# Forgetting-attention layer: the last gate projections move beside the last head, the maxima run 34 units ahead, half of w_out is split in front of the last head, the constant rows come by DMA

## The chip, the cores and the metric

One Trainium2 chip, one core of it. The metric is the time of one execution on the device in microseconds, as the median of several runs. The kernel before took 1217.65 us (three runs, 1216.58 to 1218.84).

## The reference, cut to what matters

One decoder layer over 2048 tokens of width 1024. Eight heads of forgetting attention (full causal softmax with a bias from summed gate logits) and eight query heads of sliding-window attention share one normalised input and one input projection. Each head's output is multiplied by a SiLU gate; one output projection, a norm and a gated residual follow.

```python
proj = h @ w_in[l]
qa, ka, va, fa, za, qb, kb, vb, zb = jnp.split(proj, split_points, axis=-1)
...
oa = oa * jax.nn.silu(za)
...
y = jnp.concatenate([oa, ob], axis=-1) @ w_out[l]
x = x + gate[:, None, :] * rms_norm(y, g_post[l])
```

and in forgetting_attention, for a block of 128 queries:

```python
s = jnp.einsum('bhqd,bhkd->bhqk', qb, kh, preferred_element_type=jnp.float32) * scale
s = s + cb[..., None] - cum[:, :, None, :]
...
s = jnp.where(causal, s, -jnp.inf)
p = jax.nn.softmax(s, axis=-1)
return jnp.einsum('bhqk,bhkd->bhqd', p.astype(vh.dtype), vh)
```

## The kernel before, in words

Every product is made of three f16 matmuls: operands are split into a high and a low half, and high x high, high x low and low x high are summed in PSUM. The tokens lie in four chunks of 512. `hT[0..3]` holds the normalised input of each chunk, turned and split, 16 KB a partition each.

The kernel has three stages on one instruction stream per engine. First the input is normalised and turned. Then the sliding-window stage runs, with projections between its pieces. Its last piece hands over to the third stage, the forgetting attention (FoX), whose start I call the prologue. The output projection follows at the end.

**Units.** A projection of one 128-column weight group for one chunk (`proj_units`, L299) is eight units, each of three matmuls of 512 columns (L308). The list `punits` holds all of them in order, and `fill(n)` issues the next n. `qk0..qk7` are query and key of the eight FoX heads, `za0..za3` the gates of two heads each, `va3` the last values. When a chunk of `qk` is done, ACT and DVE make its high and low half (`stq`, L997 and L990) and four DMAs on SP's queue put them into the tile `T` of the head (L992 to L995; two such tiles take turns). A chunk of `za` goes through a tanh on ACT (L352) and a product on DVE (L348), and GpSimd's queue stores it to `z_d` in DRAM (L350).

**Weights.** Each group is loaded, its largest magnitude found (DVE, L212), sent through DRAM (`mx_d`, L215 and L220, GpSimd's queue) and split (ACT L246, DVE L252), so many units ahead of its first use (`add`, L902).

**Maxima.** The softmax needs a row bound per query. `munits` holds for each head 40 segments, each a matmul on `T` (L1209) and a maximum on DVE (L1212, or L1214 on the diagonal), and four short units that turn the bound into extra rows of `T` (L1166, ACT L1170, SP L1172): 44 per head (`M_HEAD`). The first `M_LEAD` = 26 are issued in the prologue, beside its last projections.

**Steps.** A head is 20 steps, each of up to 1024 scores per query row. Step s does on ACT the exponential of its scores (L1265) and the f16 high half (L1269), on DVE the low half of the step before (L1272), on TensorE the scores of the next step (L1258, L1259, on the diagonal L1261) and the values product of the step two back (`PV_LAG` = 2, L1282 to L1285). Between them stand some filling units and 2.2 maxima a step. A head's chunk ends with a division (L1289, L1291) and a store of `ona` to `o_d` on SP's queue (L1292). In heads 0 to 6 the filling units are projections. In the last head steps 0 to 7 have none, and from step 8 on the first 33 units of the output projection (L1407) fill.

**The last head before.** After its step 0 `open_out` (L1319) closes the pools of `hT` and of the staging tiles and opens those of the output stage. `w_out` is loaded in 16 pieces of 128 x 512 on SP's queue (L1342) and split, one piece a step from step 2 on, by ACT (L1347) and DVE (L1348), right after the step's exponential. The left half (pieces 0 to 7) is needed by the first product in step 9. The loads of the first two output blocks (`o_d`, L1362, and `z_d`, L1364) follow steps 4 and 6; their turning (`Out.turn`) makes ACT square and round a gated block (L1383, L1393).

**Constant rows.** `T` needs three constant values in each row of its two slots. In the prologue four small matmuls (L1157) and sixteen ACT copies of 5 x 512 (L1159) put them there.

Of the kernel before, what the change touches and what calls it, by code (L numbers as in the profile page):

```python
# [41 lines left out]
def hybrid_layer(  # L42
# [75 lines left out]
    hpx = ExitStack()  # L118
    hpool = hpx.enter_context(tc.tile_pool(name="hpool", bufs=1))
# [13 lines left out]
    hT = [hpool.tile([P, 2, KT, CH], F16, name=f"hT{i}") for i in range(NCH)]  # L133
# [517 lines left out]
    def open_fox():  # L651
# [8 lines left out]
        fx["cst"] = cst = fxv.tile([P, 2, XR], F16, name="cst")  # L660
        for ap, val in ((vt[:, :, :, 64:65], 1.0), (cst[:], 0.0), (fx["lk"][:], 0.0), (fx["lq"][0][:], 0.0),
                        (fx["lq"][1][:], 0.0), (cst[:, 0, 64:65], XA), (cst[:, 0, 65:66], XB),
                        (cst[:, 0, 68:69], XC), (cst[:, 1, 66:67], XA), (cst[:, 1, 67:68], XB)):
            V.memset(ap, val)

# [312 lines left out]
    N_SWA = len(punits)  # L978
    for ci in range(2):
        add("va3", va_units(3, ci))  # L980
# [173 lines left out]
    def const_rows(n, slot):  # L1154

        px = bk[bank()][:]
        PE.matmul(px[0:XR, 0:P], fx["cst"][:, slot // 2, :], identh[:], start=True, stop=True)  # L1157
        for c_ in range(NCH):
            after(1, lambda c_=c_: A.activation(  # L1159
                Ts[n][64:XR, slot, c_ * CH:(c_ + 1) * CH].rearrange("p (u q) -> p u q", u=4),  # L1160
                px[64:XR, 0:P].unsqueeze(1).broadcast_to([XR - 64, 4, P]), AF.Copy))
# [149 lines left out]
    M_HEAD, M_LEAD, PV_LAG = 44, 26, 2  # L1311
# [7 lines left out]
    def open_out():  # L1319
# [5 lines left out]
        stp = foxo.enter_context(tc.tile_pool(name="stpo", bufs=6, reuse_waits="tile"))  # L1325
        oxy = foxo.enter_context(tc.tile_pool(name="oxy", bufs=2, reuse_waits="tile"))
        oio["x"] = lambda: oxy.tile([P, D], F32, tag="xr", name="xr")
        oio["y"] = lambda: oxy.tile([P, D], F32, tag="yg", name="yg")
# [10 lines left out]
    def w_out_load(m):  # L1339
        k, cc = m % KT, slice((m // KT) * CH, (m // KT + 1) * CH)  # L1340
        w_raw[m] = stp.tile([P, CH], F32, tag="st", name=f"wo{m}")
# [10 lines left out]
    class Out:  # L1352
# [43 lines left out]
        def product(self, n, k):  # L1396
# [15 lines left out]
            def evac():  # L1412
                if n == 0:
                    self.y = oio["y"]()
# [179 lines left out]
```

## Time and profile before

| | us |
|---|---|
| median of three runs | 1217.65 |
| the profiled execution | 1213.1 |
| its span, first to last instruction | 1211.3 |
| TensorE busy | 1156.8 |
| DVE busy | 907.4 |
| ACT busy | 675.1 |

The page's "busy" is the time in which an engine has an instruction under way; for TensorE (PE) ends are modelled and neighbours overlap, so its rate is read from how closely instructions start. Windows are stretches of the span with the busy time of each engine, and PEclk is the share of the full TensorE clock that was granted. In the timeline, what stands in brackets is the idle time of the engine before a row and what ended it.

### The profile page before, as it was taken

To read this page: it belongs to the slowest core of one execution; us is meant where nothing else is said; L and a number is where in the kernel's file an instruction comes from. 1 tells how busy PE (TensorE), PEld (TensorE's weight loads), DVE (VectorE), ACT (ScalarE), POOL (GpSimd) and SP (SyncE) were. 2 spreads that over 40 slices of the span, in tenths; PEclk is the share of its full clock that TensorE was granted. 3 is DMA by queue.
4 is the path that set the end of the run, shared out by engine and by line. 5 is a ranking of instruction groups with operands and counts; after the bars stand their busy time and mean duration, and the time that the engine had idled before them with its cause. 6 is when DMAs were issued, how large, how long until landed. Compare 5 with 4: busy or idle time off the path is not lost.

```text
span 1211.3 us, 27309 instructions
## 1 busy us (share of the span) xinstructions
PE 1156.8 (96%) x10832; PEld 698.7 (58%) x10832; DVE 907.4 (75%) x2271; ACT 675.1 (56%) x1117; POOL 142.1 (12%) x252
## 2 busy tenths in 40 slices
PE   6789999999999999999999999999999969999996
PEld 2467546865558976555555555555555546555553
DVE  6866567686776646688888798888978787667665
ACT  2766445565655451566667666666766779433231
POOL 2011133223232210001010110010000000000000
PEclk8889999999999999999999999999999989999998
DMA  9554332323323322313334323122111146455652
GB/s 325 189 146 142 83 95 73 86 56 102 96 68 87 57 55 51 82 58 84 84 60 83 88 61 79 38 72 53 42 45 36 41 140 192 144 164 184 202 170 81
DMA packets 87668, 120.97 MB, mean 100 GB/s; under 512 B 27340, under 2 KB 63220, under 8 KB 87540
## 3 DMA queue, kind: packets, MB, share of 16 engines
q1 hardware_dynamic: 76564, 86.20, 23.8%
q0 software_dynamic: 10976, 33.03, 11.6%
q8 instruction: 85, 1.39, 0.5%
q14 instruction: 43, 0.35, 0.1%
HBM read 71.82 MB, written 25.18 MB: 80 GB/s over the span
## 4 chain that ended last, share of the span: by engine, by line
PE 80%; DVE 7%; DMA 6%; SPq 3%; ACT 2%; issue 1%; POOL 0%; DVEq 0%; ACTq 0%; POOLq 0%
PE bk L308 30%; PE bk L1407 13%; PE bk L326 7%; PE sta L1258 4%; PE sta L1259 4%; PE bk L1209 4%; PE poa L1284 2%; PE poa L1285 2%; PE poa L1282 2%; PE pxb L866 2%; PE pss L833 2%; PE pob L885 2%; DVE pha L1272 1%; DMA xt<-in_x_dram 1%; PE bk L1370 1%
## 5 line engine op out<-in xcount | busy, mean ns | idle before, releaser
L1265 ACT ACTIVATE p<-sta,lift,scl_qk 128x1024 f32<-128x1024 f32 (+2 forms) x160 | 171.9, 1075 | 128.7 <-PE sta L1259 72.7
L308 PE MATMUL bk<-hT,wh_qk 128*128 128x512 f16 x768 | 193.4, 378 | 0.6 <-DVE a_m L1212 0.6
L1407 PE MATMUL bk<-wohl,oz 128*128 128x512 f16 x768 | 172.1, 379 | 0.0
L1272 DVE TENSOR_TENSOR pha<-p,pha 128x1024 f16<-128x1024 f32 (+2 forms) x160 | 169.1, 1057 | 0.2 <-ACT pha L1269 0.2
L1212 DVE TENSOR_REDUCE a_m<-bk 128x1 f32<-128x512 f32 x192 | 130.2, 686 | 49.7 <-PE bk L1209 49.1
L1269 ACT ACTIVATE pha<-p 128x1024 f16<-128x1024 f32 (+2 forms) x160 | 148.0, 925 | 5.5 <-PE bk L1209 0.4
L1407 PEld LDWEIGHTS <-oz 128*128 128x128 f16 x768 | 74.4, 99 | 81.2
L1282 PE MATMUL poa<-vt,pha 128*128 128x65 f16 x1088 | 117.6, 194 | 1.3 <-DVE ona L1291 1.2
L1258 PE MATMUL sta<-T 128*128 128x512 f16 (+1 forms) x320 | 111.7, 349 | 7.5 <-ACT p L1265 7.3
L1285 PE MATMUL poa<-vt,pha 128*128 128x65 f16 x1088 | 117.3, 193 | 1.1 <-DVE pha L1272 1.1
L1284 PE MATMUL poa<-vt,pha 128*128 128x64 f16 x1088 | 117.7, 195 | 0.0
L308 PEld LDWEIGHTS <-wh_qk 128*128 128x128 f16 x768 | 73.0, 97 | 76.0 <-issue 1.7
L1209 PE MATMUL bk<-T 66*128 66x512 f16 (+2 forms) x320 | 110.1, 351 | 2.9 <-DMA T<-stq 2.0
L1282 PEld LDWEIGHTS <-pha 128*128 128x128 f16 x1088 | 102.3, 97 | 16.5 <-DVE ona L1291 3.0
L1259 PE MATMUL sta<-T 69*128 69x512 f16 (+1 forms) x320 | 110.8, 351 | 0.0
L1284 PEld LDWEIGHTS <-pha 128*128 128x128 f16 x1088 | 101.7, 97 | 11.3
L1285 PEld LDWEIGHTS <-pha 128*128 128x128 f16 x1088 | 101.6, 99 | 1.3 <-DVE pha L1272 1.3
L308 PE MATMUL bk<-hT,wh_za 128*128 128x512 f16 x384 | 99.4, 378 | 0.0
L308 PE MATMUL bk<-hT,wh_zb 128*128 128x512 f16 x384 | 89.9, 379 | 1.1 <-DVE wh_zb L252 1.1
L326 PE MATMUL bk<-wh_va,hT 128*128 128x128 f16 x1536 | 90.7, 219 | 0.0
L326 PEld LDWEIGHTS <-hT 128*128 128x128 f16 x1536 | 87.5, 98 | 5.0 <-issue 2.5
L308 PE MATMUL bk<-hT,wh_qb 128*128 128x512 f16 x384 | 87.2, 379 | 0.0
(493 smaller groups left out, 1890.5 us busy)
## 6 DMA issues: line engine op xcount, KB each, us to landing
wa<-in_w_ada_dram SPq DMA_DIRECT2D x16, 512.0 KB
z_d<-tz POOLq DMA_DIRECT2D x32, 256.0 KB, 3.1
T<-stq SPq DMA_DIRECT2D x64, 128.0 KB
T<-o_d SPq DMA_DIRECT2D x16, 512.0 KB
T<-z_d SPq DMA_DIRECT2D x16, 512.0 KB
xr<-in_x_dram SPq DMA_DIRECT2D x16, 512.0 KB
out_dram<-yg SPq DMA_DIRECT2D x15, 512.0 KB
xt<-in_x_dram SPq DMA_DIRECT2D x12, 512.0 KB
```

The costliest lines, as they stand in the source:

```text
L308: PE.matmul(ps, whl[:, a, k, :], hT[ci][:, b, k, :], start=(k == 0 and n == 0), stop=(k == KT - 1 and n == 2))
L326: PE.matmul(ps[:, u * P:(u + 1) * P], hT[ci][:, a, k, u * P:(u + 1) * P], whl[:, b, k, :], start=(k == 0 and n == 0), stop=(k == KT - 1 an ...
L1209: PE.matmul(mx[:, :w], T[0:XM, 0, i * P:(i + 1) * P], T[0:XM, 2, pc * CH:pc * CH + w], start=True, stop=True)
L1258: PE.matmul(self.st[:, o:o + w], T[:, 3, kb_], T[:, 1, qc], start=True, stop=False)
L1259: PE.matmul(self.st[:, o:o + w], T[0:XR, 2, kb_], T[0:XR, 0, qc], start=False, stop=not diag)
L1265: A.activation(self.p32[:, :self.w], self.st[:, :self.w], AF.Exp, scale=scl[f"qk{self.hd}"][:], bias=lift[:])
L1269: A.activation(self.ph[:, 0, :self.w], self.p32[:, :self.w], AF.Copy)
L1272: V.tensor_tensor(self.ph[:, 1, :self.w], self.p32[:, :self.w], self.ph[:, 0, :self.w], op=ALU.subtract)
L1282: PE.matmul(po[:, u, :], ph[:, 0, pq], vt[:, b, hd, 0:65], start=(self.first and n == 0 and u == 0), stop=False)
L1284: PE.matmul(po[:, u, 0:64], ph[:, 0, pq], vt[:, b, hd, 65:VW], start=False, stop=False)
L1285: PE.matmul(po[:, u, :], ph[:, 1, pq], vt[:, b, hd, 0:65], start=False, stop=(self.last and n == len(self.blocks) - 1))
L1407: PE.matmul(py, self.hl[:, i, k, :], w_slot(8 * j + k)[:, cc], start=(k == 0 and m_ == 0), stop=(k == KT - 1 and m_ == 2))
```

## The change

It has five parts.

1. **Gates.** The filling list keeps `qk1..qk7` and the gates of heads 0 to 6 in heads 0 to 6 (336 units up to `N_LAST` instead of 352). The last two chunks of `za3` (16 units) follow `N_LAST` and are issued two a step in steps 0 to 7 of the last head. In the list, `qk7`'s chunks stand between those of `za3`, and the weights of the `za` groups are prepared against a due place moved by four units (for `za3` by 20).
2. **Maxima.** `M_LEAD` is 34 instead of 26: eight more units are issued in the prologue, from 14 units before `N_QK0` on instead of 10. Each head's key rows are made at steps 0 and 1 instead of 2 and 3.
3. **w_out.** `open_out` happens when all but the last chunk of `qk7` and nothing late is pending (it comes in step 12 of the head before the last). It closes only `hT[0]` and `hT[1]`. The left half's eight pieces are split in steps 14 to 19 of that head and in steps 1 and 3 of the last head, the right half's in steps 9 to 16 of the last head. Each piece is loaded once, two steps ahead (before, piece 0 was loaded twice, after steps 0 and 1).
4. **Buffers.** `hT[2]` and `hT[3]` stay. The right half's pieces land in `hT[3]`, and the two residual and two output tiles of the output stage lie in `hT[2]`. The staging pool there has 4 tiles instead of 6.
5. **Constant rows.** One matmul and one ACT copy, 40 units before the end of the sliding-window list, make a row tile `crow`. In the prologue three DMAs per `T` spread it, on SP's queue for `T[0]` and on ACT's queue for `T[1]`.

```diff
-    for hd in range(1, 9):
+    for hd in range(1, 7):
         for part in range(6):
             if part in (3, 5):
                 add(f"za{(hd - 1) // 2}", za_units(hd - 1, (part - 3) // 2))
-            elif hd < 8:
+            else:
                 add(f"qk{hd}", qk_units(hd, (0, 1, 2, 0, 3)[part]))
+    add("qk7", qk_units(7, 0))
+    add("za3", za_units(6, 0))
+    add("qk7", qk_units(7, 1))
+    add("qk7", qk_units(7, 2))
+    add("za3", za_units(6, 1))
+    N_OPEN = len(punits)
+    add("qk7", qk_units(7, 3))
+    N_LAST = len(punits)
+    for n in range(2):
+        add("za3", za_units(7, n))
...
-            at = len(punits) - (24 if key[:2] == "za" else 0)
+            at = len(punits) - {"za3": 4}.get(key, 20 if key[:2] == "za" else 0)
...
-    def const_rows(n, slot):
-        px = bk[bank()][:]
-        PE.matmul(px[0:XR, 0:P], fx["cst"][:, slot // 2, :], identh[:], start=True, stop=True)
-        for c_ in range(NCH):
-            after(1, lambda c_=c_: A.activation(
-                Ts[n][64:XR, slot, c_ * CH:(c_ + 1) * CH].rearrange("p (u q) -> p u q", u=4),
-                px[64:XR, 0:P].unsqueeze(1).broadcast_to([XR - 64, 4, P]), AF.Copy))
+    def const_rows(n, eng):
+        for slot, r0, r1 in ((0, 64, 66), (2, 66, 68), (0, 68, 69)):
+            eng.dma_start(Ts[n][r0:r1, slot, :].rearrange("p (u q) -> p u q", q=P),
+                          fx["crow"][r0:r1, :].unsqueeze(1).broadcast_to([r1 - r0, NB, P]))
...
-    M_HEAD, M_LEAD, PV_LAG = 44, 26, 2
+    M_HEAD, M_LEAD, PV_LAG = 44, 34, 2
...
-            if mi < M_LEAD and pos[0] >= N_QK0 - 10:
+            if mi < M_LEAD and pos[0] >= N_QK0 - 14:
...
-        p0, p_tot = pos[0], len(punits) - pos[0]
+        p0, p_tot = pos[0], N_LAST - pos[0]
-        w_at = {r: [r - 2] if r < 10 else [8, 9] if r == 10 else [r - 1] for r in range(2, 17)}
+        w_at, opened = {}, False
...
+            if hd == 7 and r < 8:
+                npn = N_LAST + (len(punits) - N_LAST) * (r + 1) // 8 - pos[0]
...
-            if hd == 7 and r == 0:
+            if not opened and pos[0] >= N_OPEN and (r >= 14 or not late):
+                while late:
+                    tick()
                 open_out()
-            if hd == 7:
-                for m in (w_at[2] if r == 1 else []) + w_at.get(r + 2, []):
-                    w_out_load(m)
+                opened = True
+                here = list(range(s + 2, 7 * NS))[:KT]
+                here += [7 * NS + n for n in (1, 3, 5, 7, 8)][:KT - len(here)] + [7 * NS + n for n in range(9, 17)]
+                w_at = {t: [m] for m, t in enumerate(here)}
+            for m in w_at.get(s + 2, []):
+                w_out_load(m)
```

Three places show how the instructions move. First ACT's row at the start of the prologue, before (`T` are the tiles of two heads, `rw` the key rows of head 0, `stq` the chunks of `qk0`):

```order
L1098 ACTIVATE wsq,a_m<-wsq 128x256
L1159 ACTIVATE T_6650<-bk_134 5x512 x4
L1159 ACTIVATE T_6650<-bk_136 5x512 x4
L1159 ACTIVATE T_6651<-bk_135 5x512 x4
L1159 ACTIVATE T_6651<-bk_6625 5x512 x4
L1170 ACTIVATE rw<-bk_6626 48x128
L997 ACTIVATE stq<-bk_134 128x512
```

The same place now; the sixteen copies are gone and three DMA issues stand there, the other three being in SP's row:

```order
L1118 ACTIVATE wsq,a_m<-wsq 128x256
L1177 DMA T_6657<-crow 2x16x128 x2
L1177 DMA T_6657<-crow 1x16x128
L1187 ACTIVATE rw<-bk_137 48x128
L1006 ACTIVATE stq<-bk_138 128x512
```

Second, ACT's row from step 19 of head 6 into the last head, before (`p` is an exponential, `pha` its high half, `wohl` a split piece of w_out):

```order
L1265 ACTIVATE p_14138<-sta,lift,scl_qk_11693 128x384
L1269 ACTIVATE pha<-p_14138 128x384
L1265 ACTIVATE p_14184<-sta,lift,scl_qk_12666 128x896
L1269 ACTIVATE pha<-p_14184 128x896
L1265 ACTIVATE p_14245<-sta,lift,scl_qk_12666 128x384
L1269 ACTIVATE pha<-p_14245 128x384
L1170 ACTIVATE rw<-bk_6625 8x128
L1265 ACTIVATE p_14279<-sta,lift,scl_qk_12666 128x1024
L1347 ACTIVATE wohl<-wo_14275,wsc 128x512
L1269 ACTIVATE pha<-p_14279 128x1024
```

The same engine now, in steps 14 to 17 of head 6; the splits begin eight steps sooner, one a step:

```order
L1282 ACTIVATE p_13905<-sta,lift,scl_qk_11874 128x1024
L1368 ACTIVATE wohl<-wo_13864,wsc 128x512
L1286 ACTIVATE pha<-p_13905 128x1024
L1006 ACTIVATE stq<-bk_6632 128x512
L1282 ACTIVATE p_13953<-sta,lift,scl_qk_11874 128x1024
L1368 ACTIVATE wohl<-wo_13903,wsc 128x512
L1286 ACTIVATE pha<-p_13953 128x1024
L1282 ACTIVATE p_14000<-sta,lift,scl_qk_11874 128x1024
L1368 ACTIVATE wohl<-wo_13951,wsc 128x512
```

Third, SP's queue around the first loads of w_out, before (`o_d_72<-ona` is the store of head 6's last chunk):

```order
L1342 DMA wo_14243<-in_w_out_dram 128x512
L1172 DMA T_6651<-rw 2x4x128
L1292 DMA o_d_72<-ona 128x4x64
L1342 DMA wo_14275<-in_w_out_dram 128x512
L1342 DMA wo_14277<-in_w_out_dram 128x512
L1342 DMA wo_14319<-in_w_out_dram 128x512
L1292 DMA o_d_69<-ona 128x4x64
```

The same queue now; the second and third load stand behind the store of head 6's third chunk, and the eighth behind that of its last:

```order
L1359 DMA wo_13864<-in_w_out_dram 128x512
L1309 DMA o_d_71<-ona 128x4x64
L1359 DMA wo_13903<-in_w_out_dram 128x512
L1359 DMA wo_13951<-in_w_out_dram 128x512
L1001 DMA T_6657<-stq 64x2x512
```

```order
L1189 DMA T_6657<-rw 2x4x128
L1359 DMA wo_14095<-in_w_out_dram 128x512
L1359 DMA wo_14181<-in_w_out_dram 128x512
L1309 DMA o_d_72<-ona 128x4x64
L1359 DMA wo_14262<-in_w_out_dram 128x512
```

In both fences a load that stood behind a store of `ona` keeps one in front of it, but now only three of the left half's eight do.

More of the change, by code (lines that the diff above doesn't have):

```diff
@@ L131, in hybrid_layer @@
     swc = swx.enter_context(tc.tile_pool(name="swc", bufs=1))
-    hT = [hpool.tile([P, 2, KT, CH], F16, name=f"hT{i}") for i in range(NCH)]
+    hT = [(hpool if i < 2 else hlate).tile([P, 2, KT, CH], F16, name=f"hT{i}") for i in range(NCH)]
     cosT = swc.tile([P, S], F32, name="cosT")
@@ L659, in open_fox, with const_turn @@
         fx["lq"] = [fxv.tile([P, LW], F16, name=f"lq{n}") for n in range(2)]
-        fx["cst"] = cst = fxv.tile([P, 2, XR], F16, name="cst")
+        fx["cst"] = cst = fxv.tile([P, XR], F16, name="cst")
+        fx["crow"] = fxv.tile([P, P], F16, name="crow")
         for ap, val in ((vt[:, :, :, 64:65], 1.0), (cst[:], 0.0), (fx["lk"][:], 0.0), (fx["lq"][0][:], 0.0),
-                        (fx["lq"][1][:], 0.0), (cst[:, 0, 64:65], XA), (cst[:, 0, 65:66], XB),
-                        (cst[:, 0, 68:69], XC), (cst[:, 1, 66:67], XA), (cst[:, 1, 67:68], XB)):
+                        (fx["lq"][1][:], 0.0), (cst[:, 64:65], XA), (cst[:, 65:66], XB),
+                        (cst[:, 66:67], XA), (cst[:, 67:68], XB), (cst[:, 68:69], XC)):
             V.memset(ap, val)
+    def const_turn():
+        px = bk[bank()][:]
+        PE.matmul(px[0:XR, 0:P], fx["cst"][:], identh[:], start=True, stop=True)
+        after(1, lambda: A.activation(fx["crow"][64:XR, :], px[64:XR, 0:P], AF.Copy))
     def va_units(j, ci):
@@ L1472, in hybrid_layer @@
         V.tensor_copy(cmask[:, 3 * P:], dmask[:])
-        for n in range(2):
-            for slot in (2, 0):
-                const_rows(n, slot)
-                tick()
+        const_rows(0, SP)
+        const_rows(1, A)
         key_limbs(0)
```

28 lines of the change are left out of this document (16 added, 12 removed).

## The prediction

> **What bounds the kernel now.** I read the page first, then windows cut at the stages of FoX, then the timeline at the two places where TensorE stops. In the page's row each engine has its busy time:
>
> ```profile
> PE 1156.8 (96%) x10832; PEld 698.7 (58%) x10832; DVE 907.4 (75%) x2271; ACT 675.1 (56%) x1117; POOL 142.1 (12%) x252
> ```
>
> TensorE is the bound on average, so time can only come from where it stops. The windows show where; per row: length, busy time of PE, its weight loads, DVE, ACT, POOL, then the granted clock.
>
> ```profile
> core 0: us, PE busy (x) PEld busy (x) DVE busy (x) ACT busy (x) POOL busy (x), PEclk, DMA share, GB/s
> 441.30:444.70 3.40, 1.26 (x15) 0.77 (x12) 2.76 (x15) 3.38 (x9) 0.71 (x1) 1.00 0.14 43
> ...
> 559.90:630.20 70.30, 68.95 (x705) 39.47 (x702) 61.11 (x136) 46.27 (x54) 6.12 (x10) 1.00 0.27 66
> 630.20:907.40 277.20, 276.58 (x2809) 159.35 (x2806) 236.09 (x523) 183.05 (x212) 20.80 (x33) 1.00 0.28 62
> ...
> 957.30:973.50 16.20, 14.46 (x225) 9.76 (x222) 15.31 (x30) 13.93 (x18) 0.54 (x1) 1.00 0.09 34
> 973.50:977.50 4.00, 2.98 (x37) 1.44 (x34) 3.61 (x10) 1.17 (x1) 0.00 (x0) 1.00 0.09 24
> 977.50:982.60 5.10, 0.00 (x0) 0.00 (x0) 2.05 (x5) 2.81 (x4) 0.00 (x0) 0.65 0.50 166
> 982.60:992.70 10.10, 9.86 (x102) 6.20 (x102) 10.01 (x19) 8.44 (x12) 0.00 (x0) 0.67 0.53 158
> 992.70:1009.90 17.20, 14.32 (x152) 10.00 (x149) 16.00 (x30) 15.60 (x21) 0.00 (x0) 0.90 0.79 248
> 1009.90:1037.00 27.10, 27.10 (x288) 16.16 (x287) 19.39 (x27) 23.93 (x33) 0.00 (x0) 1.00 0.37 120
> ```
>
> Heads 2 to 5 (630.2 to 907.4) are TensorE's: 276.58 of 277.20 us, DVE at 85%. From step 15 of head 6 (957.3) to step 10 of the last head (1009.9) it is otherwise: 52.6 us with 41.62 us of PE, no projections being left to fill with. I call this stretch E. Part of its PE time is slow as well:
>
> ```profile
> 982.60:985.90 3.30, 3.24 (x19) 1.73 (x19) 3.27 (x7) 2.91 (x4) 0.00 (x0) 0.50 0.00 0
> 985.90:989.20 3.30, 3.30 (x34) 2.40 (x33) 3.25 (x7) 2.13 (x4) 0.00 (x0) 0.50 0.68 196
> ...
> 999.50:1002.90 3.40, 3.26 (x34) 2.86 (x33) 3.33 (x7) 3.13 (x4) 0.00 (x0) 0.50 0.55 158
> ```
>
> These 9.8 us ran at half clock and would be 4.9 at full, so E holds 36.7 us of PE work and loses 15.9. Its longest stop, in timelines of SP, ACT and PE:
>
> ```profile
> 957.27 1.21 ACT L1265 ACTIVATE p<-sta,lift,scl_qk 128x1024 f32<-128x1024 f32 x1 [0.59 <-PE sta L1259]
> ...
> 976.22 0.37 SPq L1292 DMA_DIRECT2D o_d<-ona  x1
> 976.63 1.46 SPq L1342 DMA_DIRECT2D wo<-in_w_out_dram  x3
> 979.79 0.72 ACT L1347 ACTIVATE wohl<-wo,wsc 128x512 f16<-128x512 f32 x1 [5.12 <-DMA wo<-in_w_out_dram]
> 982.60 0.58 PE L1258 MATMUL sta<-T 128*128 128x512 f16 x1 [5.11 <-ACT p L1265]
> ...
> 984.50 1.10 ACT L1265 ACTIVATE p<-sta,lift,scl_qk 128x896 f32<-128x896 f32 x1 [0.39 <-PE sta L1261]
> ```
>
> SP's queue stood at the store of head 6's last chunk until 976.22. The w_out loads behind it left at 976.63, and ACT, in order, waited 5.12 us for a piece before it could go on to the exponentials that TensorE needed. The half clock follows that stop.
>
> **The change part by part.** The sum is made against the profiled execution, 1213.1 us (span 1211.3 and 1.8 around it). The median is 1217.65, 4.55 above it; I carry the difference over. About 0.2%, 2.4 us, is what a measurement can tell from no change.
>
> The prices of one instruction, from the prologue's timeline (first row: start, length) and the groups by line (busy, mean ns):
>
> ```profile
> 444.68 14.41 PE L308 MATMUL bk<-hT,wh_qk 128*128 128x512 f16 x66
> L308 PE MATMUL bk<-hT,wh_za 128*128 128x512 f16 x384 | 99.4, 378 | 0.0
> L1212 DVE TENSOR_REDUCE a_m<-bk 128x1 f32<-128x512 f32 x182 | 123.5, 686 | 48.7 <-PE bk L1209 48.1
> L1348 DVE SCALAR_TENSOR_TENSOR wohl<-wo,wsc,wohl 128x512 f16<-128x512 f32 x16 | 11.9, 748 | 6.3 <-ACT wohl L1347 6.3
> L1347 ACT ACTIVATE wohl<-wo,wsc 128x512 f16<-128x512 f32 x16 | 11.3, 714 | 8.8 <-DMA wo<-in_w_out_dram 8.8
> L352 ACT ACTIVATE tz<-bk,cz_za 128x512 f32<-128x512 f32 x16 | 10.9, 683 | 4.6 <-PE bk L308 4.6
> L348 DVE SCALAR_TENSOR_TENSOR tz<-tz,bk 128x512 f32<-128x512 f32 x16 | 10.9, 679 | 0.0
> ```
>
> A matmul of 512 columns costs TensorE (14.41 - 0.38) / 65 = 0.216 us, a filling unit of three 0.65 us.
>
> *Gates, heads 0 to 6.* Two chunks, 48 matmuls, leave the place where TensorE is the bound: 48 x 0.216 = 10.4 us less. What is late next there is DVE, whose share of heads 2 to 5 goes from 85% to 87%. At 87% head 1 (559.9 to 630.2) lost 1.35 us a head, heads 2 to 5 lost 0.6 in four. If all six heads lost 1.35, the stops would grow by some 6 us; if none did, by 0. Head 1's stretch also carries the adaLN gate's products, so I stay nearer the four heads: +1.0. Together -9.4.
>
> *Gates and w_out, stretch E.* I count each engine in the two halves of E. First half, step 15 to step 3 of the last head, 957.3 to 984.5, 27.2 us. DVE worked 15.31 + 3.61 + 2.05 and all of the last 1.9, 22.9 us, splits of two pieces in it; now seven stand there: + 5 x 0.75 = 26.6. PE had 14.46 + 2.98 and 1.0 at full clock, 18.4, and gets eight filling units, 5.2: 23.6. ACT had 13.93 + 1.17 + 2.81 + 1.6 = 19.5 and gets 5 x 0.71: 23.1. So DVE becomes the bound of this half. It may end a step behind, so I take 25.5 (23.6 to 27): -1.7. Second half, steps 4 to 10, 984.5 to 1009.9, 25.4 us. PE had 36.7 - 18.4 = 18.3, gets eight units, 5.2, and loses eight maxima, some 1.6: 21.9. ACT had 8.44 + 15.60 less the 1.6 above, 22.4; six splits go (4.3), two tanhs come (1.4): 19.5. DVE had 24.1, loses 4.5 of splits and 8 x 0.69 of maxima and gets two products: 15.5. PE bounds it, with stops where ACT squares and rounds the first two output blocks after steps 6 and 8:
>
> ```profile
> L1383 ACT ACTIVATE zj<-T 128x1024 bf16<-128x1024 f32 x4 | 4.2, 1049 | 7.9 <-DVE T L1379 7.9
> ```
>
> Between 990 and 1050 ACT lost 7.9 us before those squares, waiting for a gated block. With fewer loads beside it I leave 2 us of stop: 23.9 (21.9 to 25.4), -1.5. The 5.12 us wait and the half clock are gone in this, because each piece is now loaded two steps ahead: a load took 979.79 - 976.63 = 3.2 us, two steps are 5 us or more. E together: -3.2. After 1009.9 TensorE is busy 27.10 of 27.10 and nothing is moved: 0.
>
> *Maxima, prologue.* Eight units come here, 1.6 us of PE work (they are in E's loss). TensorE issues the first one after 54 matmuls of `qk0` instead of 66, 12 x 0.216 = 2.6 us sooner. It needs head 0's rows in `T` (timeline; the sixth row is from the chain that ended last, start and length):
>
> ```profile
> 441.85 7.80 ACT L1159 ACTIVATE T<-bk 5x512 f16<-5x512 f32 x16
> 450.06 0.60 ACT L997 ACTIVATE stq<-bk 128x512 f16<-128x512 f32 x1
> 450.69 0.69 DVE L990 SCALAR_TENSOR_TENSOR stq<-bk,stq 128x512 f16<-128x512 f32 x1 [6.15 <-ACT stq L997]
> 452.80 0.59 POOL L215 DMA_DIRECT2D mx_d<-w_mx  x1 [9.85 <-DVE w_mx L212]
> 452.88 0.60 SPq L994 DMA_DIRECT2D T<-stq  x1
> 452.88 8.08 DMA T<-stq
> 461.10 0.22 PE L1209 MATMUL bk<-T 66*128 66x128 f16 x1 [2.01 <-DMA T<-stq]
> ```
>
> The third of the four row DMAs, issued at 452.88, landed 8.08 us later, and TensorE waited 2.01 us. If it lands at the same time, the wait grows to 4.6: +2.6. It can leave 0.8 sooner now, the two key row DMAs being through before. If it then took the 3.2 us of a w_out load, there would be no wait: -2.0. I take +2.0, since the 8.08 is the row of this very DMA. The store of `mx_d` by GpSimd's queue left 0.08 us before it, so the two were under way together. [...] Three of the 34 units find no filling unit left (31 iterations have one): each costs DVE 0.69 against 0.22 on PE, 3 x 0.4 = +1.2 (0.5 to 2).
>
> *Constant rows.* Sixteen copies of together 7.80 us leave ACT, but they were hidden: `qk0` began at 444.68, and its first chunk (24 x 0.216 = 5.2) was not ready for ACT before 449.9, the copies ending at 449.65. TensorE's start at 444.68 waits for the key limbs on DVE, which was busy 2.76 of the 3.40 us before. Three small matmuls fewer: -0.4 to 0. The six DMAs go ahead of the key rows on SP and ACT, which are not needed before 450: 0, and 2 us if one were late. I take -0.2. *Buffers*: as many tiles of each kind as before, 0; the fewer staging tiles cost at most one 0.7 us split behind DVE.
>
> Sum: -9.4 - 3.2 + 1.6 + 2.0 + 1.2 - 0.2 = -8.0. The profiled execution would be 1205.1, the median 1209.6.
>
> **The rivals.** *The clock falls in the prologue.* TensorE's wait there becomes 4.6 us and the clock halves, as after the 5.11 us stop. Then 6.6 us at half clock cost 3.3, and with the wait's other 0.6 the time is 1213.5. For it: the two waits are of one size. Against it: at 977.5 the stretch ahead had already been thin (2.98 of 4.00), here PE is full until the wait. [...]
>
> *DVE becomes the bound of heads 0 to 6*, and the 10.4 us are not given back but for some 3: 1209.6 + 7.4 = 1217, no change. For it: the 87% and the 1.35 us of head 1. Against it: 0.6 us of stops in four heads at 85%.
>
> *Slower: ACT waits for w_out twice.* Pieces 1 and 2 now stand on SP's queue behind the store of head 6's third chunk, and piece 7 behind that of its last. If each such store comes so late that its load lands five us after ACT wants it, there are two stops of 5.1 us, each with 3.3 us of half clock: 1209.6 + 16.8 = 1226. It decides where such a store leaves later than two steps (5 us or more) less 3.6 us (its issue and the load) after its place. For it: this very order made the 5.12 us. Against it: before, the split came one step after the store, now two.
>
> *The rows of `T` come in time*, and DVE has slack all through: -4.0 in the prologue, -1.0 in the heads: 1204.6.
>
> That the change does not do what it says can be left aside: the moved instructions stand in the order shown.
>
> **How the numbers follow.** The forecast has 0.56, with 1205 to 1214 as its own range; the clock in the prologue 0.17 at 1213.5; DVE in heads 0 to 6 0.13 at 1217; the two waits 0.07 at 1226; rows in time 0.07 at 1204.6. The range that leaves out 2 in 10 goes from 1203.5 to 1217.5: the forecast, the first two rivals and the last, without their ends. Faster means under 1215.2: 0.53 of the forecast, 0.14 of the clock's case, 0.01 of DVE's, 0.07 of the last, 0.75. Slower means over 1220.1: the two waits and little else, 0.08. Between: 0.17.
>
> **What would show it.** Right: heads 2 to 5 about 6 us shorter with PE still over 99% busy; no stop of PE over 2 us between step 15 of head 6 and step 10 of the last head, and no half clock there; DVE the fullest engine in the last five steps of head 6; the wait at the first maximum 4 us or so. Wrong: stops on DVE in heads 2 to 5, ACT waiting on `wo` before a split, the clock at half after 456, or a stretch E over 52 us.

## The result, and the profile after

The changed kernel takes 1211.5 us (median of 7 runs, 1208.4 to 1212.9), the kernel before 1217.65 (7 runs, 1214.6 to 1219.3): a ratio of 0.9948, 95% interval 0.9932 to 0.9965, so 6 us faster. The forecast was 1209.6. On a second chip the changed kernel's ratio was 0.9965 (0.9953 to 0.9977).

The two profiled executions don't show that difference as a whole: 1211.0 us of span beside 1211.3. The profiled execution of before lies under all its timed runs, that of after is the slowest of its seven. So I compare stretches, cut at the last matmul of the sliding stage and at exponentials, and take a second profile of the changed kernel, from the second chip, beside the first. The rows of E end where the next step's exponential starts.

| stretch, us | before | after | second profile | change | forecast |
|---|---|---|---|---|---|
| prologue, to the first exponential | 42.7 | 50.3 | 48.4 | +7.6, +5.7 | +4.6 |
| heads 0 to 6, to step 15 of head 6 | 473.1 | 463.9 | 464.9 | -9.2, -8.2 | -9.4 |
| E, first half (through step 3 of the last head) | 27.2 | 28.0 | 27.1 | +0.8, -0.1 | -1.7 |
| E, second half (steps 4 to 10) | 25.4 | 22.6 | 22.6 | -2.8 | -1.5 |
| the rest | 201.4 | 200.9 | 200.9 | -0.5 | 0 |
| together | 769.8 | 765.6 | 763.8 | -4.2, -6.0 | -8.0 |

The sliding stage ended at 441.5 before, at 445.4 and 446.0 after. Little of that can be the change's: in ten profiles of kernels whose instructions are the same up to there it ended between 442.4 and 448.8, and in a second profile with the order of before at 444.6.

The page's row of busy times, and the windows of after, columns as before (length, PE, weight loads, DVE, ACT, POOL, clock):

```profile
PE 1153.7 (95%) x10829; PEld 696.0 (57%) x10829; DVE 908.2 (75%) x2271; ACT 662.0 (55%) x1102; POOL 142.1 (12%) x252
```

```profile
core 0: us, PE busy (x) PEld busy (x) DVE busy (x) ACT busy (x) POOL busy (x), PEclk, DMA share, GB/s
445.40:448.60 3.20, 0.48 (x4) 0.38 (x4) 2.76 (x15) 0.35 (x2) 0.71 (x1) 1.00 0.21 54
448.60:495.70 47.10, 42.58 (x331) 25.36 (x332) 28.45 (x80) 6.77 (x13) 4.55 (x7) 0.93 0.23 45
...
638.60:910.20 271.60, 270.65 (x2783) 156.78 (x2780) 236.20 (x522) 180.15 (x211) 20.83 (x33) 1.00 0.27 61
959.60:974.20 14.60, 10.74 (x171) 7.12 (x168) 14.24 (x27) 12.43 (x18) 0.00 (x0) 1.00 0.45 133
974.20:987.60 13.40, 13.09 (x123) 7.16 (x120) 12.08 (x23) 8.69 (x12) 0.00 (x0) 1.00 0.11 31
987.60:1010.10 22.50, 20.03 (x239) 13.18 (x239) 16.91 (x31) 20.19 (x26) 1.08 (x2) 1.00 0.71 221
```

Heads 2 to 5 took 277.2 us and take 271.6, with PE still at 99.6%: the 5.6 us that 26 matmuls fewer (2809 to 2783) were to give, 26 x 0.216. In the last five steps of head 6 (959.6 to 974.2) DVE is busy 14.24 of 14.60 us. The prologue is the surprise: 4.5 us of its 47.1 without PE work, and a clock of 0.93. TensorE's timeline there, the rows that carry an idle time:

```profile
446.97 0.38 PE L1123 MATMUL bk<-w_mx,ones 128*128 128x1 f32 x2 [1.55 <-DVE w_mx L1121]
448.52 0.25 PE L1183 MATMUL bk<-identh,lk 128*72 128x128 f16 x1 [1.17 <-DVE lk L1203]
...
461.95 0.22 PE L1226 MATMUL bk<-T 66*128 66x128 f16 x1
...
465.86 0.39 PE L1226 MATMUL bk<-T 66*128 66x512 f16 x1 [0.60 <-DVE a_mr L1245]
...
475.56 0.39 PE L1226 MATMUL bk<-T 66*128 66x512 f16 x1 [2.21 <-DMA T<-stq]
...
490.71 0.25 PE L1183 MATMUL bk<-identh,lq 128*72 128x128 f16 x1 [0.49 <-DVE lq L1246]
...
494.38 0.38 PE L1226 MATMUL bk<-T 66*128 66x512 f16 x1 [1.23 <-DVE a_m L1229]
```

The first maximum (461.95) waits for nothing. The fifth (465.86) and the thirteenth (475.56) wait; they are the first ones on the second and third chunk of rows (three expectations below call the thirteenth the tenth). At the fifth this profile names DVE, the second one the row DMA (1.35 us). The last two stops are maxima with no filling left between them. By the distance of starts these four stops are 0.76, 2.37, 0.65 and 1.39 us; the second profile has 1.51, 1.40, 0.65 and 1.39. Before, there were 2.17 and 0.42.

The clock falls twice, each time for 3.41 us. Windows cut at those times:

```profile
445.40:448.81 3.41, 0.69 (x5) 0.48 (x5) 2.76 (x15) 0.35 (x3) 0.71 (x1) 1.00 0.20 52
448.81:452.23 3.42, 3.42 (x10) 1.21 (x9) 0.00 (x0) 0.27 (x1) 0.00 (x0) 0.50 0.04 7
472.70:476.11 3.41, 1.20 (x7) 0.41 (x5) 1.54 (x7) 0.00 (x0) 0.46 (x1) 1.00 0.15 8
476.11:479.52 3.41, 3.41 (x27) 2.67 (x25) 1.26 (x2) 0.86 (x2) 0.09 (x1) 0.50 0.36 41
```

Each is a stretch in which PE worked, at half clock, after one in which it stood for 2.7 and 2.2 us of 3.4. The second profile has one such window in the prologue, before's had none.

In stretch E the 5.12 us wait is gone, but waits for w_out are not (the waits of ACT in E: us in total, times, longest; then its timeline):

```profile
ACT wohl L1368 <- DMA wo<-in_w_out_dram: 4.6, 3, 2.5
```

```profile
962.25 0.72 ACT L1368 ACTIVATE wohl<-wo,wsc 128x512 f16<-128x512 f32 x1 [1.49 <-DMA wo<-in_w_out_dram]
...
985.99 0.72 ACT L1368 ACTIVATE wohl<-wo,wsc 128x512 f16<-128x512 f32 x1 [2.50 <-DMA wo<-in_w_out_dram]
```

TensorE stopped 2.2 us after the first and 1.57 after the second. No window of E is at half clock in this profile, one is in the second.

### The profile page after: what moved, and what is told of

Read it like the earlier page. It is cut to its first block, busy times and chain, and to the rows that moved or that the text cites. A ratio compares the mean times of both kernels' runs of the same rounds, so it can differ in the third digit from the quotient of the medians.

```text
span 1211.0 us, 27262 instructions
## 1 busy us (share of the span) xinstructions
PE 1153.7 (95%) x10829; PEld 696.0 (57%) x10829; DVE 908.2 (75%) x2271; ACT 662.0 (55%) x1102; POOL 142.1 (12%) x252
## 3 DMA queue, kind: packets, MB, share of 16 engines
q8 instruction: 85, 1.39, 0.6%
## 4 chain that ended last, share of the span: by engine, by line
PE 53%; DVE 4%; ACT 1%; DMA 1%; issue 1%; SPq 0%; DVEq 0%; ACTq 0%
PE bk L309 17%; PE bk L1428 14%; PE sta L1276 4%; PE sta L1275 4%; PE bk L1226 4%; PE poa L1301 2%; PE poa L1302 2%; PE poa L1299 2%; DVE a_m L1229 1%; PE bk L1391 1%; DMA wo<-in_w_out_dram 1%; DVE pha L1289 1%; DMA T<-stq 1%; PE sta L1278 1%; ACT p L1282 0%
## 5 line engine op out<-in xcount | busy, mean ns | idle before, releaser
L309 PE MATMUL bk<-hT,wh_qk 128*128 128x512 f16 x768 | 198.2, 381 | 0.0
L1299 PE MATMUL poa<-vt,pha 128*128 128x65 f16 x1088 | 116.4, 193 | 1.9 <-DVE ona L1308 1.9
L1302 PE MATMUL poa<-vt,pha 128*128 128x65 f16 x1088 | 116.0, 192 | 1.3 <-DVE pha L1289 1.0
L309 PE MATMUL bk<-hT,wh_za 128*128 128x512 f16 x384 | 99.3, 378 | 0.0
```

The costliest lines, as they stand in the source:

```text
L309: PE.matmul(ps, whl[:, a, k, :], hT[ci][:, b, k, :], start=(k == 0 and n == 0), stop=(k == KT - 1 and n == 2))
L1299: PE.matmul(po[:, u, :], ph[:, 0, pq], vt[:, b, hd, 0:65], start=(self.first and n == 0 and u == 0), stop=False)
L1302: PE.matmul(po[:, u, :], ph[:, 1, pq], vt[:, b, hd, 0:65], start=False, stop=(self.last and n == len(self.blocks) - 1))
```

## The experiments

My theory is the forecast's sum, each term from its own cause. The rivals are that the clock makes the prologue's loss, that E is bound by something else than DVE, and that the lead costs more than it gives. "Ratio" is to the kernel before on the same chip.

**The changed kernel again.** No edit.

> The changed kernel once more, unaltered, as the yardstick of the other runs on this chip: ratio to the kernel before 0.993 to 0.997. Its profile is a second look at the prologue, 445 to 496 in the first, which took 7.6 us longer there than before, against 4.6 in the forecast. Theory 1, the clock falls because of stops that the change itself makes (3.1 us without work ahead of qk0, 2.2 us at the tenth maximum): two windows of 3.4 us at half clock again, 47 us from the first matmul of qk0 to the first exponential. Theory 2, the half clock there was chance of that execution: none, 43.5 to 44 us.

Ratio 0.9965 (0.9953 to 0.9977). From qk0's first matmul to the first exponential 45.2 us, one window at half clock (450.4 to 453.9) instead of two. Neither theory as put: the half clock is neither fixed nor absent. The next runs show what decides it.

**Gates back in heads 0 to 6.**

```diff
+    for n in range(2):
+        add("za3", za_units(7, n))
     N_LAST = len(punits)
-    for n in range(2):
-        add("za3", za_units(7, n))
...
-            if not opened and pos[0] >= N_OPEN and (r >= 14 or not late):
+            if not opened and s >= 6 * NS + 12 and pos[0] >= N_OPEN and (r >= 14 or not late):
```

> The last two gate chunks stand in heads 0 to 6 again (48 matmuls of 0.216 us), all else as changed, w_out opened in the same step. Forecast's terms: heads 0 to 6 longer by 9.4 us, stretch E shorter by some 2 (its second half lacks 5.2 us of filling, but 2 of it were stops that filling covers; its first half is DVE's), together 7 us slower than the changed kernel, 1218.5. Rival A, E is not bound by DVE or ACT and the filling is paid for in full there: E shorter by 5, together 4 us slower, 1215.5. Rival B, the gain of heads 0 to 6 comes from the maxima ahead and not from the gates: no change, 1211.5.

1218.2 us, ratio 1.0010 (0.9996 to 1.0023), beside the changed kernel's 1211.7 on that chip: 6.4 us slower. Heads 0 to 6 took 473.1 us, before's number, and the two halves of E:

```profile
963.90:991.00 27.10, 19.47 (x274) 12.29 (x271) 26.50 (x50) 21.81 (x27) 0.54 (x1) 1.00 0.27 84
991.00:1012.60 21.60, 17.49 (x221) 12.48 (x221) 15.74 (x29) 19.40 (x24) 0.00 (x0) 0.92 0.72 227
```

The forecast's term holds and both rivals fall: 8 to 9 us in the heads, against 1 us in E's second half. That half has one window at half clock here (0.92), worth up to 1.7 us, so its 1 us is a lower bound. In the first half the 5 us of filling cost nothing: DVE is busy 26.50 us of it without them, 26.3 and 26.0 with them.

**26 maxima ahead.**

```diff
-    M_HEAD, M_LEAD, PV_LAG = 44, 34, 2
+    M_HEAD, M_LEAD, PV_LAG = 44, 26, 2
...
-            if mi < M_LEAD and pos[0] >= N_QK0 - 14:
+            if mi < M_LEAD and pos[0] >= N_QK0 - 10:
```

> 26 maxima ahead, as before the change, all else as changed. Forecast's terms: the prologue shorter by 4.8 us (8 units 1.6, wait for rows 2.0, unfilled units 1.2), the eight units come back in the last head, +1.6: together 3.2 us faster than the changed kernel, 1208.3. Rival A, from the changed kernel's profile, where the prologue took 7.6 us more with two windows at half clock: if the lead makes all of that, 7.6 - 1.6 = 6 us faster, 1205.5. Rival B, the stops of the prologue stay, being due to the weight maximum of za0 and to the chain of the key limbs: only the eight units and the unfilled ones move, about 1 us faster, 1210.5.

1204.3 us, ratio 0.9903 (0.9891 to 0.9916): 7.5 us faster than the changed kernel, the most of any single edit. Its prologue and its E, halved:

```profile
447.70:486.20 38.50, 38.50 (x323) 23.47 (x323) 23.13 (x65) 6.62 (x12) 3.33 (x6) 0.96 0.22 46
```

```profile
949.90:977.00 27.10, 23.28 (x280) 14.51 (x277) 25.40 (x47) 21.00 (x28) 0.00 (x0) 0.94 0.26 78
977.00:1003.00 26.00, 24.25 (x267) 14.95 (x264) 21.55 (x42) 20.37 (x26) 1.08 (x2) 1.00 0.62 182
```

No stop is left after qk0 has begun (38.50 of 38.50). The prologue is 6.7 us shorter than in the changed kernel's second profile, E 3.5 longer, nearly all of it in the second half. By the stretches that is 4.4 us against the second profile and 6.2 against the first; rival A is nearest, rival B falls.

**The weight preparation of za0 later.**

```diff
-            at = len(punits) - {"za3": 4}.get(key, 20 if key[:2] == "za" else 0)
+            at = len(punits) - {"za3": 4, "za0": 4}.get(key, 20 if key[:2] == "za" else 0)
```

> The weight preparation of za0 is moved 16 units later (its 1.21 us maximum on DVE and its store to mx_d leave the stretch in which the rows of qk0's third chunk are made), all else as changed. In the changed kernel TensorE stops 2.37 us (second look: 1.40) before the tenth maximum, for those rows. Theory 1, DVE is late by the 1.21 us and the store holds the rows up by another 1: that stop goes, 1.4 to 2.4 us faster than the changed kernel, up to 1.7 more where a half clock followed it. Theory 2, the lead itself makes the stop (the unit is asked for before its rows can be there): the stop stays over 1 us, no change in time within 1 us. 34 maxima stay, so with either theory the kernel stays over 4 us slower than with 26, which ran at 0.9903 of the kernel before.

1215.1 us, ratio 0.9985 (0.9974 to 0.9996): slower, which neither theory had. The stop at the thirteenth maximum went, but one of 6.6 us came at the fifth. Timelines of POOL, SP and PE:

```profile
458.01 0.90 POOL L207 DMA_DIRECT2D wr_za<-in_w_in_dram  x1
...
462.80 0.60 SPq L1004 DMA_DIRECT2D T<-stq  x1
...
470.87 0.61 PE L1226 MATMUL bk<-T 66*128 66x512 f16 x1 [6.60 <-DMA T<-stq]
```

The edit moved the load of za0's raw weights too (128 x 1024 in f32, half a megabyte), to 458.01, 2.5 to 5 us ahead of that chunk's row DMAs. The last of these left at 462.80, and TensorE waited for them until 470.87, 8 us. In the changed kernel's two profiles the same chunk, with the load elsewhere, was used 2 to 3 us after its last DMA had left. So for the time the edit was not the clean test that it was meant to be. For the thirteenth maximum it tells something: the store of za0's maximum, 1.7 us ahead of the third chunk's row DMAs in the changed kernel, does not leave before 482 here, and TensorE had these rows without a stop at 480.08, 2.2 us after the last of the DMAs had left (477.92). In the changed kernel they landed 5.0 to 6.4 us after their issue.

**Eight units of qk0 first.**

```diff
+        fill(8, tick2)
         key_limbs(0)
         key_rows(0)
-        fill(8, tick2)
```

> The first eight units of qk0 (24 matmuls, 5.2 us) are issued ahead of the key limbs and key rows of head 0, all else as changed. In the changed kernel TensorE does 3.1 us of nothing between the last matmul of the sliding stage (445.4) and qk0 (448.6), waiting for the limbs on DVE, and the next 3.4 us run at half clock. Theory 1: both go, 2.7 + 1.7 = 4.4 us faster, 1207.1. Theory 2, the half clock there was chance: 2.7 us faster, 1208.8. Rival: the key rows now leave 5 us later and the first maximum, which came without a wait at 461.95, waits for them 2 to 3 us: no change, 1211.

1210.4 us, ratio 0.9946 (0.9924 to 0.9967), 1.4 us faster in the median, not to be told from no change. qk0 starts at once (445.44, the sliding stage ending at 445.6), but the prologue is as long as in the changed kernel's second profile, 48.1 us. The rival holds: the first maximum waits for the key rows (`rw`), and the rows of the third chunk follow the earlier TensorE as little at the thirteenth:

```profile
459.98 0.22 PE L1226 MATMUL bk<-T 66*128 66x128 f16 x1 [2.52 <-DMA T<-rw]
...
475.21 0.39 PE L1226 MATMUL bk<-T 66*128 66x512 f16 x1 [2.52 <-DMA T<-stq]
```

**The kernel before, one store on another queue.**

```diff
-                SP.dma_start(o_d[self.ci][:, hd * 64:(hd + 1) * 64].rearrange("(u p) d -> p u d", p=P), on[:])
+                (G if (hd, self.ci) == (6, 3) else SP).dma_start(o_d[self.ci][:, hd * 64:(hd + 1) * 64].rearrange("(u p) d -> p u d", p=P), on[:])
```

> The kernel before, with one edit: the store of the last chunk of head 6 goes by GpSimd's queue and no longer by SP's, so the first loads of w_out don't stand behind it. Theory 1 (forecast): ACT's 5.12 us wait and the 9.8 us at half clock in stretch E (52.6 us) come from that store; they go, and what is left is DVE's work, 47 us, and its waits: 3 to 5 us faster than the kernel before, 1213. Rival A, stretch E is bound by ACT and DVE whatever TensorE's clock is: the wait moves to later steps, under 1 us faster. Rival B, the loads are slow by themselves (four at once): the wait shrinks to 3 us, 2 us faster.

1213.0 us, ratio 0.9968 (0.9955 to 0.9981): 3.9 us faster than the kernel before (2.3 to 5.5), by one line. E is 49.8 us instead of 52.6; the first half went from 27.2 to 23.8, the second from 25.4 to 26.0. The half clock did not go:

```profile
978.70:982.10 3.40, 1.47 (x25) 0.85 (x24) 3.37 (x10) 2.56 (x3) 0.76 (x1) 1.00 0.65 211
982.10:988.90 6.80, 6.50 (x51) 4.08 (x51) 6.75 (x13) 5.10 (x8) 0.00 (x0) 0.50 0.33 80
```

ACT still waited 1.69 us for the first piece, and TensorE stood 1.84 us there instead of 5.27, in a window that was thin anyway. Theory 1 holds for the size and for most of the wait, not for the clock.

**The left half of w_out in the last head.**

```diff
-                here = list(range(s + 2, 7 * NS))[:KT]
+                here = [7 * NS + n for n in range(1, 9)]
```

> The left half of w_out is split in steps 1 to 8 of the last head, one piece a step, each loaded two steps ahead; nothing of it is split in head 6; all else as changed. Theory 1 (forecast): the first half of E is DVE's, so it gets shorter by up to 1.9 us when five splits leave it, and the second half longer by 1 to 2 (ACT gets 3.5 us more): no change within 1 us, E 49 to 51 us. Rival A, the early splits are where E's gain comes from: E longer by 3 us or more, 1214.5. Rival B, the stops of the changed kernel at steps 17 to 19 of head 6 (2.2 and 1.2 us) come from the splits there: they go with them, 2 us faster, 1209.5.

1209.6 us, ratio 0.9945 (0.9930 to 0.9961). From the end of the sliding stage on it took 764.2 us, between the two profiles of the changed kernel (765.6, 763.8). E's halves:

```profile
954.80:979.70 24.90, 23.16 (x294) 14.34 (x291) 23.40 (x44) 19.44 (x23) 0.00 (x0) 1.00 0.24 65
979.70:1005.70 26.00, 22.53 (x243) 14.70 (x242) 20.51 (x36) 22.77 (x32) 1.08 (x2) 0.93 0.77 249
```

DVE loses 2.6 to 2.9 us in the first half and the half loses 2.2 to 3.1; the second gets 3.4 longer, up to 1.7 of it by a window at half clock (0.93). What the early splits give, they take: theory 1.

**Constant rows by ACT copies.** The functions `const_rows` and their calls as in the kernel before.

> The constant rows by four matmuls and sixteen ACT copies as in the kernel before, all else as changed. Forecast: the copies lie beside TensorE's first 5.2 us of qk0, and three small matmuls weigh nothing: 0 to 0.4 us slower than the changed kernel. Theory 2: the four matmuls kept TensorE from standing idle for a whole window of 3.4 us ahead of qk0, and without them the clock is at half in the next window (in three of five looks at kernels that have the DMAs, in none of one at the kernel before): up to 1.7 us faster, no half clock between 445 and 455.

1212.6 us, ratio 0.9972 (0.9954 to 0.9989): no difference. Theory 2 falls: with the four matmuls there the clock fell all the same.

```profile
443.20:446.61 3.41, 1.49 (x25) 1.00 (x20) 2.59 (x15) 3.38 (x9) 0.71 (x1) 1.00 0.15 43
446.61:450.03 3.42, 3.19 (x9) 1.27 (x10) 0.17 (x1) 3.42 (x8) 0.00 (x0) 0.51 0.00 0
```

The run with the gates back, in turn, had the same 3.1 us of standing and no half clock. There the standing lies across two windows:

```profile
442.36:445.77 3.41, 2.25 (x52) 2.12 (x49) 1.13 (x4) 1.00 (x3) 0.41 (x1) 1.00 0.03 6
445.77:449.18 3.41, 1.85 (x10) 1.06 (x11) 1.63 (x12) 0.27 (x1) 0.30 (x1) 1.00 0.20 51
```

**26 maxima and the eight units first.** Both edits above.

> 26 maxima ahead and the first eight units of qk0 ahead of the key limbs and rows, all else as changed. With 26 alone the kernel ran at 0.9903 of the kernel before; with 34, the eight units ahead saved 3.1 us of standing and lost most of it again to a wait of 2.68 us at the first maximum and of 2.68 at the tenth. Theory 1, these waits belong to the early start of the maxima: with 26 the first maximum comes 2.6 us later and finds its rows; 3 us faster than 26 alone, 4.7 if a window at half clock goes too: 0.9865 to 0.988. Theory 2, they belong to the rows of the key limbs, which now leave 5 us later: the wait stays, 0.9895 to 0.9905.

1200.8 us, ratio 0.9860 (0.9845 to 0.9876): the fastest version with the next one, 17 us under the kernel before. Theory 1, a little under its range; no window from qk0 to the end of E is at half clock. TensorE goes from the sliding stage into qk0 without a gap, and the first maximum waits a quarter of a microsecond:

```profile
443.07 0.86 PE L893 MATMUL pob<-vb,ptb 128*128 128x64 f16 x24
443.77 2.32 PE L309 MATMUL bk<-hT,wh_qk 128*128 128x512 f16 x10
...
458.63 0.22 PE L1226 MATMUL bk<-T 66*128 66x128 f16 x1 [0.26 <-DMA T<-stq]
```

Its prologue is 37.4 us with PE busy 37.14, beside 50.3 and 48.4.

**That, and the left half late.** With the edit to `here` above as well.

> The kernel with 26 maxima ahead and the eight units first, and the left half of w_out split in steps 1 to 8 of the last head instead of from head 6 on. With 34 maxima this move left stretch E as it was (50.9 us beside 49.7 and 50.5). With 26, the second half of E has eight more maxima, so DVE and ACT are fuller there. Theory 1, the place of the splits is of no account as long as each load is two steps ahead: within 1.5 us of the kernel without this edit. Theory 2 (forecast: the splits ahead of the last head relieve the second half): 2 to 3 us slower than that.

Ratio 0.9861 (0.9840 to 0.9881), the same. E is 50.2 us instead of 51.7 (23.6 and 26.7 instead of 25.7 and 26.0). Theory 1; the forecast's reason for early splits falls.

**Stores of `ona` off SP's queue.** To the kernel with 26 and eight first.

```diff
-                SP.dma_start(o_d[self.ci][:, hd * 64:(hd + 1) * 64].rearrange("(u p) d -> p u d", p=P), on[:])
+                (G if hd == 6 and self.ci > 1 else SP).dma_start(o_d[self.ci][:, hd * 64:(hd + 1) * 64].rearrange("(u p) d -> p u d", p=P), on[:])
```

> The kernel with 26 maxima ahead and the eight units first, and the stores of head 6's third and last chunk on GpSimd's queue instead of SP's. In the changed kernel ACT waited 1.49 us for a piece of w_out that stood behind the first of them and 2.50 for one behind the second, and TensorE stopped 2.2 and 1.57 us there. Theory 1, the stores make these waits: both stops go, 2 to 3 us faster than without this edit. Rival, the loads would be late anyway, or GpSimd's queue with the store delays the z_d stores: within 1 us.

Ratio 0.9890 (0.9873 to 0.9906), E 52.5 us instead of 51.7; from the end of the sliding stage on the two took the same, 754.7 and 754.5 us. ACT's waits for w_out in E, here and then without this edit:

```profile
ACT wohl L1368 <- DMA wo<-in_w_out_dram: 1.4, 1, 1.4
ACT wohl L1368 <- DMA hT<-in_w_out_dram: 1.0, 1, 1.0
```

```profile
ACT wohl L1368 <- DMA wo<-in_w_out_dram: 1.5, 2, 1.2
ACT wohl L1368 <- DMA hT<-in_w_out_dram: 1.1, 1, 1.1
```

The rival holds: the pieces come late without the stores ahead of them too. The medians are 3.5 us apart. Of the 5.0 us between the two profiled executions, 4.9 arose before the sliding stage's end, in instructions that are the same; why, stays open. So a few us between single kernels may come from there, and the stretches are the safer comparison.

**34 maxima, but started later.** `N_QK0 - 10` with `M_LEAD` 34, a single run, so only its profile counts.

> 34 maxima ahead, but the first is issued from 10 units before the end of qk0 on as before the change (not 14); all else as changed. It parts the early start from the number. The changed kernel's prologue has stops of 0.76 and 2.37 us at maxima that wait for rows, and 2.0 where maxima stand without filling between them. Theory 1: the stops for rows go (under 0.5 us together) and eight units without filling instead of four make 3 to 4 us, the prologue 1 us shorter than the changed kernel's 47.1 from the first matmul of qk0. Theory 2, the rows are late whatever the start: stops of 2 us or more at rows remain.

Not one stop at rows, and 2.94 and 0.54 us of stops at the end:

```profile
489.48 0.25 PE L1183 MATMUL bk<-identh,lq 128*72 128x128 f16 x1 [2.78 <-DVE lq L1246]
490.67 1.44 PE L1226 MATMUL bk<-T 66*128 66x512 f16 x3 [0.38 <-DVE a_m L1229]
```

From qk0 on it took 46.3 us beside 47.1 and 45.2, at a clock of 0.91 beside 0.93 and 0.96. Theory 1 for the stops: the early start makes the waits for rows, the number makes the unfilled ones, and either way the lead costs TensorE time. The length lies between the changed kernel's two.

## Why the prediction was right, and where it was not

The time came within 2 us of the forecast and inside its range. Not all terms held, and part of the closeness is luck: in E the two halves missed in opposite ways (-2.0 and -2.9 together beside -3.2), and the prologue came out near its +4.6 in the second profile from other stops than those that were added up.

- **Gates, heads 0 to 6, -9.4:** -9.2 and -8.2; putting them back gave 473.1 us again. DVE at 87% did not bind: the rival that it would falls. TensorE was the bound there (99.6 and 99.3% busy in heads 2 to 5), and most of the 10.4 us of 48 matmuls came back.
- **E, first half, -1.7:** +0.8 and -0.1. The step that failed is "It may end a step behind, so I take 25.5": I had added up 26.6 us for DVE and then taken a time below that sum. DVE was busy 26.3 and 26.0 us, as added up, and the half took 28.0 and 27.1. In the runs DVE fills 94 to 98% of this half (26.50 of 27.10, 25.40 of 27.10, 23.40 of 24.90).
- **The 5.12 us wait and the half clock:** the cause was the store, but the two together were not worth 10 us. Without the store in front, the first half is 3.4 us shorter and the second 0.6 longer, and the clock still fell. The change then filled that half with splits and got nothing there. That the wait would be gone because "each piece is now loaded two steps ahead" failed too: 4.6 us of smaller waits took its place. The piece of the 2.50 us wait left only at 981.94, behind the store of head 6's last chunk at 981.52, when ACT wanted it at 983.49. In the kernel with 26 maxima and eight units first, moving the stores away left 1.4 + 1.0 us of such waits where there had been 1.5 + 1.1.
- **E, second half, -1.5:** -2.8. With 26 maxima ahead it took 26.0 us instead of 22.6, with the left splits in it 26.0 as well, without the gates 21.6. I had PE at 21.9 us and 2 us of stops; PE was busy 20.0 us, and 21.2 in the second profile, with 2.5 and 1.4 us of stops.
- **Prologue, +1.6 + 2.0 + 1.2 - 0.2:** +7.6 and +5.7. The eight units are the 1.6. The wait moved from the first maximum, which found its rows, to the fifth and thirteenth, 3.1 and 2.9 us beside 2.6 before: +0.5 where I had +2.0. I followed only the first unit that uses rows, and I kept its 8.08 us although I had seen that the DMA could leave 0.8 us sooner: it now left 0.70 us ahead of the store of `mx_d` (457.72 and 458.42) where it had left 0.08 behind it, and landed in 2.4 us. The later chunks' rows left behind a store (last section). The unfilled maxima cost 2.0, not 1.2. And two windows at half clock (1.7 us each) in one profile, one in the other: 1.6 + 0.5 + 2.0 + 3.4 = 7.5, and 1.6 + 0.3 + 2.0 + 1.7 = 5.6. The rival of the falling clock was right in kind, and I had priced it for the wrong stop.
- **Constant rows, -0.2:** nothing. From the last matmul of the sliding stage to qk0's first it was 3.19 us before and is 3.19 after.
- **Slower by two waits for w_out:** both waits came, 1.49 and 2.50 us of ACT instead of 5.1 each. The rows in time were half right: the first were, later ones were not. Of the signs of being right, the wait of 4 us at the first maximum did not come, and one stop in E was 2.2 us. Two signs of being wrong showed: ACT waited on `wo` before splits, and in the first profile the clock was at half after 456.

So the change is the gates' 8 to 9 us and 2 to 3 in E, less 6 to 8 in the prologue. The eight maxima ahead are a loss by themselves: forecast +4.8 in the prologue against 1.6 later, measured 6.7 to 8.6 against 2.5 to 3.5.

What held the row DMA 8.08 us in the kernel before has no run of its own, but the landings that the traces record point at the store of `mx_d` (last section): of the first chunk's four row DMAs the two that left ahead of the store at 452.80 landed in 2.5 and 2.1 us, the two behind it in 8.1 and 7.6. The store at 452.80 is that of a `qk` group's weight maximum; za0's left 1.0 us after the DMA in question.

## What to carry to other kernels

Put a stretch at no less than the busy time of its fullest engine (E's first half: 26.3 us of DVE, 28.0 long), and before moving work ahead of a stop, look whether the engine that must do it has any room in the place where it lands. When a unit that needs a DMA is moved forward, follow every later unit that needs the next chunk as well, since the producer's place in the other engine's row has not moved, and look which stores to DRAM leave just ahead of its DMA (8.08 us to its landing with one 0.08 us ahead, 2.4 with it 0.70 us behind). A gap at a hand-over (3.1 us here) is closed by the next stage's independent work only if what that work overtakes is not needed sooner for it: with 34 maxima closing it gave 1.4 us, not to be told from none, with 26 it gave 5 (ratios 0.9903 and 0.9860).

## What the runs showed of the hardware

**The clock goes by windows.** In the profiles of before and after the granted clock changes on a grid of 3.41 us: each stretch between two changes is a whole number of times that long, from 1 to 253. Leaving out the first 130 us and the last 11, it fell twice in each, at 979.02 and 999.50 and at 448.83 and 476.13. In the window before each fall TensorE had stood idle for 2.0, 2.3, 2.7 and 2.2 us; the most idle time that these two profiles have in a window followed by a full one was 1.24 us. Of the windows of other runs above, those with 1.9 us of standing had one at half clock behind them (1.49 and 1.47 of work, then 0.51 and 0.50), and that with 1.56 had not (1.85 of work, then 1.00). At half clock TensorE started a matmul of 512 columns every 0.427 us (after, from 448.83) and at full clock every 0.216, so by my estimate a half-clock window that it fills costs 3.41 x (1 - 0.216 / 0.427) = 1.7 us. Three of the four falls lasted one window. The one at 979.02 lasted three, the third after a half-clock window with 0.23 us of idle time, and why stays open. The same 3.1 us stop was followed by half clock where it stood within one window (0.69 us of work, then 0.50) and not where it lay across two (2.25 and 1.85, then 1.00).

**Row DMAs beside a store of a weight maximum landed late.** The store of `mx_d` is 512 bytes, from 128 partitions to DRAM. GpSimd's next DMA, which reads it back, waited 6.84 and 7.14 us for its landing, and TensorE's stops ended within 0.25 us of that (before, 461.10 and 461.31; after, 475.56 and 475.65). GpSimd's row of before, then rows of SP and GpSimd of after:

```profile
461.31 1.11 POOL L220 DMA_DIRECT2D mxr<-mx_d  x2 [6.84 <-DMA mx_d<-w_mx]
```

```profile
457.72 0.60 SPq L1003 DMA_DIRECT2D T<-stq  x1
458.42 0.59 POOL L216 DMA_DIRECT2D mx_d<-w_mx  x1 [11.54 <-DVE w_mx L213]
461.48 0.60 SPq L1001 DMA_DIRECT2D T<-stq  x1
...
467.43 0.55 POOL L216 DMA_DIRECT2D mx_d<-w_mx  x1 [8.42 <-DVE w_mx L213]
469.15 0.62 SPq L1001 DMA_DIRECT2D T<-stq  x1
475.65 0.54 POOL L221 DMA_DIRECT2D mxr<-mx_d  x1 [7.14 <-DMA mx_d<-w_mx]
```

By the landings in the traces of before and after, the four such stores of the two prologues took 7.0 to 8.0 us. The row DMAs of `stq` that left there from 0.05 us ahead of a store to 5.4 us behind it (15) landed 7.2 to 8.7 us after the store; those with no store so near (17) landed 2.0 to 3.1 us after their own issue, ten of them within 2.4. No run moved such a store by itself (the run with za0 later moved a load too), and why the store takes 7 us, none shows.

**Rows behind a weight load were used late, too.** With half a megabyte of `wr_za` issued 2.5 to 5 us ahead, row DMAs into `T` were used 8 us after the last had left; without it, in the changed kernel, after 2 to 4.4. The store of 457.43 had landed by 465.67 there, when GpSimd began to read it back, and TensorE waited for the rows until 470.87. The load and the waiting stand together in one run, and what joins them none shows.
